# A first-weight split moved between x rows, a feed-forward block's weight sums moved into the projection before it, and a product split into the weights' old buffers

## The chip, the cores and the metric

The kernel runs on one core of a Trainium2 chip. The metric is the device time of one execution in microseconds (us); lower is better. The core has a matrix engine (TensorE, PE in the profile; its weight loads are PEld), three engines for elementwise work (VectorE = DVE, ScalarE = ACT, GpSimd = POOL) and a queue engine (SyncE = SP) that issues most DMAs. Each engine runs its own instructions in the order that the program gives it, and waits for the others through semaphores.

## The reference, cut to what matters

One encoder layer over 512 positions and 16 meta tokens, 1024 channels, all in float32:

```
h    = rmsnorm(x) ; proj = h @ w_in            # 40 column blocks of 128
a    = neighbourhood attention(proj) @ w_na_out
b    = differential attention(proj) @ w_diff_out
m    = sigmoid(g_na) * a + sigmoid(g_df) * b
x    = x + m @ w_o                             # "output projection"
h    = rmsnorm(x)
x    = x + (silu(h @ w_gate) * (h @ w_up)) @ w_down    # D_FF = 2816 = 22 * 128
out  = rmsnorm(x)[:, N_META:]
```

## The kernel before, in words

Activations lie transposed: channels on the 128 partitions, positions along the free dimension. Every float32 operand is split into a rounded high part and the remainder (`hi` by a cast on ACT, `lo` by a subtraction on DVE: `split`, lines 154 and 155; `wsplit`, lines 117 and 118, for weights), and `mm3` multiplies three times, high by high, high by low, low by high (lines 140, 142, 144).

**Order.** The kernel is written in Tile, which traces the Python program, then orders the instructions of each engine by a simulation of its own: the place in the program is a priority, and an engine takes the first instruction in that order whose inputs and whose buffers are there. So an instruction may run well ahead of its place in the code. Once ordered, an engine keeps its order on the chip. A tile of a pool shares `bufs` slots with the others of its tag; a new tile waits until a slot's last reader is done. `issue_after` pins a few instructions behind another one.

**Start** (`setup`). Column block 0 of `w_in` comes in two halves (`w0`) between the first rows of x (`xr`, eight rows of 128 channels). Each half is split (`wsplit(0, 2)`), and each x row is multiplied by the norm's gain into `xh` (ACT, line 244) and `xl` (DVE, line 245). The first dense block (tile `pk`) then runs over the rows k = 0 to 7: step k needs row k of `xh` and `xl`, and steps 4 to 7 need the second half of the weight. Two small loads (`lv` = the lambdas, broadcast to all partitions, and `mask`) are issued from POOL. `pq`, with the weight of block 1, follows `pk`.

**Weights of the dense part.** `wnext` hands out the splits of column blocks: loads three ahead into `wraw` (3 slots), splits one ahead into `whi`/`wlo` (2 slots each).

**Output projection** (`phase_b`, loop over m = 0 to 7, tile `po`). After each m: `x1[m]` gets the product added (line 854), `x_operands` makes the split operands of the feed-forward's left side (`xbh`, `xbl`, from `xg` and `xt`; line 998 and lines 1003 to 1015), `sum_sq` adds the square of `x1[m]` to `ssq` (squares on ACT, adds on POOL, the last on DVE).

**Feed-forward, gate and up** (22 blocks f). Each block forms two 512 x 128 by 128 products per half with seven multiplications of half size instead of eight (a Strassen-Winograd scheme; operands PB11, PB21, PB22, PT1 to PT4, tiles `pa`, `pb`, `pc`). `f_load(f)` loads gate weights into `fG` (a `wraw` slot) and up weights into `fV`, `fW`; `f_prep(f)` makes the sums of them and splits four operands: g = gate (`whi`/`wlo`), w (`fwh`/`fwl`, 2 slots), s (`fsh`/`fsl`, 1 slot), d (`fdh`/`fdl`, 1 slot). `f_products(f)` issues the seven products; in block 0 the mean of squares (`ms`, line 181) stands in product PT4. `glu` forms `g[f]` = silu(gate) * up. In the loop f, the preparation of block f + 1 is written ahead of the products of block f.

**Down projection** (tile `pdn`). `gh`, `gl` are the split of the 22 `g`; blocks (0, k) and (1, k) alternate over k, then m = 2 to 7. The pieces of `w_down` are split by `d_ahead`: the first two into `whi`/`wlo`, the others into a ring that takes the place of `xbh`/`xbl` (`wring`). Before, the 22 `gh` are a pool of their own (`GH`) opened when the pool of the feed-forward weights (`F`) is closed.

## Time and profile before

| | us |
|---|---|
| median of 3 runs (772.54 to 774.10) | 773.04 |
| the profiled execution, its own time | 773.11 |
| its span, first to last instruction | 771.3 |
| PE busy in the span | 748.6 |
| DVE / ACT / POOL busy | 575.6 / 379.7 / 55.3 |

The profile page lists busy time by engine, the span in slices, the chain of work that ended last, and groups of instructions. Beside it there is the timeline: start, duration, engine, line, operation, output tile <- input tiles, shape, count of merged instructions; in brackets, the idle time of the engine just before, and what ended it. The windows view gives busy time (and number of instructions) per engine in a stretch, and the granted TensorE clock as a share of full speed (PEclk).

### The profile page before, as it was taken

The page shows a single profiled execution, that of the slowest core. Times are in us where ns is not written, and L with a number is a line of the kernel's source. Part 1 is how long each engine was busy: PE and PEld are TensorE (multiplying, and loading weights), DVE is VectorE, ACT ScalarE, POOL GpSimd, SP SyncE. Part 2 cuts the span into 40 slices and gives each one's busy share as a digit, 9 for nine tenths or more (in the row PEclk, how much of TensorE's full clock was granted, in tenths as well). Part 3 has the DMA queues.
Part 4 walks back from the last instruction along what each step waited for, and adds up shares of the span by engine and source line. Part 5 has one row for each costly group of instructions (what it writes and reads, how often), then busy time and mean ns, then how long its engine had stood idle before and what let it go on. Part 6 is the DMA issues. An engine that isn't in the chain of part 4 may idle for free.

```text
span 771.3 us, 12598 instructions
## 1 busy us (share of the span) xinstructions
PE 748.6 (97%) x4794; PEld 674.1 (87%) x4794; DVE 575.6 (75%) x1053; ACT 379.7 (49%) x669; POOL 55.3 (7%) x141
## 2 busy tenths in 40 slices
PE   7999999999999999999998999999999989999995
PEld 5899889998889888878887999999999987888884
DVE  5777897788788867648889899999999959632214
ACT  6345545545554546514554655555555556422201
POOL 2030110110011000001121000000000000000100
PEclk8999999999999999999998999999999999999998
DMA  7474643453563412235541333333333232633003
GB/s 261 136 182 143 158 123 103 123 152 104 137 159 101 121 58 80 82 110 163 169 132 42 110 110 110 110 107 104 104 104 108 66 102 68 206 103 95 1 1 109
DMA packets 34715, 87.88 MB, mean 114 GB/s; under 512 B 4512, under 2 KB 6576, under 8 KB 34656
## 3 DMA queue, kind: packets, MB, share of 16 engines
q1 hardware_dynamic: 32688, 82.97, 35.6%
q0 software_dynamic: 1136, 3.34, 1.5%
q8 instruction: 37, 0.61, 0.3%
q10 hardware_dynamic: 832, 0.79, 0.3%
q14 instruction: 22, 0.18, 0.1%
HBM read 70.01 MB, written 2.10 MB: 93 GB/s over the span
## 4 chain that ended last, share of the span: by engine, by line
PE 85%; DVE 9%; DMA 2%; issue 1%; ACT 1%; SPq 0%; DVEq 0%; ACTq 0%
PE pdn L144 4%; PE pdn L140 4%; PE pdn L142 4%; PE pa L140 4%; PE pa L144 4%; PE pb L140 4%; PE pg L140 4%; PE pa L142 4%; PE pb L142 4%; PE pb L144 4%; PE pg L144 4%; PE pg L142 4%; PE s L513 2%; PE pv L140 2%; PE pv L142 2%; PE pv L144 2%
## 5 line engine op out<-in xcount | busy, mean ns | idle before, releaser
L117 ACT CAST whi<-wraw 128x1024 fp32r<-128x1024 f32 (+1 forms) x57 | 58.9, 1033 | 56.9 <-PE pd L142 13.1
L118 DVE TENSOR_TENSOR wlo<-wraw,whi 128x1024 fp32r<-128x1024 f32 (+1 forms) x57 | 68.5, 1201 | 17.2 <-ACT whi L117 16.9
L144 PE MATMUL pdn<-gh,wring 128*128 128x512 f32 x138 | 53.8, 390 | 1.3 <-DVE wring L155 1.3
L140 PE MATMUL pdn<-gh,wring 128*128 128x512 f32 x138 | 53.8, 390 | 0.0
L142 PE MATMUL pdn<-gl,wring 128*128 128x512 f32 x138 | 53.7, 389 | 0.0
L140 PE MATMUL pg<-xh,whi 128*128 128x512 f32 x128 | 52.6, 411 | 0.4 <-DVE vt L379 0.4
L142 PE MATMUL pg<-xl,whi 128*128 128x512 f32 x128 | 50.6, 395 | 0.0
L144 PE MATMUL pg<-xh,wlo 128*128 128x512 f32 x128 | 50.2, 393 | 0.0
L155 DVE TENSOR_TENSOR wring<-draw,wring 128x1024 fp32r<-128x1024 f32 (+1 forms) x22 | 24.7, 1126 | 28.8 <-ACT wring L154 28.8
L154 ACT CAST wring<-draw 128x1024 fp32r<-128x1024 f32 (+1 forms) x22 | 21.0, 974 | 45.9 <-PE pdn L142 34.5
L154 ACT CAST fdh<-fG 128x1024 fp32r<-128x1024 f32 x22 | 23.2, 1056 | 36.8 <-PE pa L142 34.7
L154 ACT CAST ath<-tp 128x256 fp32r<-128x256 f32 (+1 forms) x48 | 20.5, 443 | 42.2 <-PE tp L637 22.0
L1137 POOL TENSOR_TENSOR ssq<-ssq,sq 128x512 f32<-128x512 f32 x11 | 16.4, 1493 | 345.6 <-ACT sq L1136 335.2
L155 DVE TENSOR_TENSOR wlo<-fG,whi 128x1024 fp32r<-128x1024 f32 x22 | 26.9, 1224 | 14.4 <-ACT whi L154 14.4
L517 ACT ACTIVATE e<-s,m 128x528 f32<-128x528 f32 x32 | 22.5, 704 | 23.0 <-DVE m L515 22.7
L144 PEld LDWEIGHTS pdn<-gh,wring 128*128 128x128 f32 x138 | 25.9, 188 | 7.1 <-DVE wring L155 1.7
L140 PE MATMUL pk<-xh,whi 128*128 128x256 f32 (+1 forms) x128 | 28.9, 303 | 3.1 <-ACT xh L244 3.1
L140 PEld LDWEIGHTS pdn<-gh,wring 128*128 128x128 f32 x138 | 25.9, 188 | 5.6 <-ACT wring L154 0.2
L142 PEld LDWEIGHTS pdn<-gl,wring 128*128 128x128 f32 x138 | 25.9, 188 | 5.3
L155 DVE TENSOR_TENSOR fwl<-fW,fwh 128x1024 fp32r<-128x1024 f32 x22 | 26.9, 1225 | 3.1 <-ACT fwh L154 3.1
L144 PEld LDWEIGHTS pg<-xh,wlo 128*128 128x128 f32 x128 | 24.0, 188 | 5.2
L621 ACT ACTIVATE en<-en,m 128x272 f32<-128x272 f32 x32 | 16.7, 522 | 24.1 <-DVE m L619 23.8
(292 smaller groups left out, 2596.2 us busy)
## 6 DMA issues: line engine op xcount, KB each, us to landing
wraw<-in_w_in_dram SPq DMA_DIRECT2D x39, 512.0 KB, 3.8
fG<-in_w_gate_dram SPq DMA_DIRECT2D x22, 512.0 KB, 3.5
kd<-khl SPq DMA_DIRECT2D x32, 264.0 KB, 4.2
draw<-in_w_down_dram SPq DMA_DIRECT2D x16, 512.0 KB, 3.6
fW<-in_w_up_dram SPq DMA_DIRECT2D x22, 256.0 KB, 2.6
fV<-in_w_up_dram SPq DMA_DIRECT2D x22, 256.0 KB, 2.9
qs<-qhl SPq DMA_DIRECT2D x32, 128.0 KB, 2.8
wraw<-in_w_o_dram SPq DMA_DIRECT2D x8, 512.0 KB, 3.5
```

What stands on the lines that cost most here:

```text
L117: nc.scalar.copy(hi[:, k:k + h], raw[:, k:k + h])
L118: eng.tensor_tensor(out=lo[:, k:k + h], in0=raw[:, k:k + h], in1=hi[:, k:k + h].bitcast(F32), op=ALU.subtract)
L140: nc.tensor.matmul(outs[i], wh, rhs[i][0], start=start, stop=False, **kw)
L142: nc.tensor.matmul(outs[i], wh, rhs[i][1], start=False, stop=False, **kw)
L144: nc.tensor.matmul(outs[i], wl, rhs[i][0], start=False, stop=stop, **kw)
L154: self.nc.scalar.copy(hi, src)
L155: self.nc.vector.tensor_sub(lo, src, hi.bitcast(F32))
L513: nc.tensor.matmul(sc[:, r0:r1], qs[:, q], kd[:, p, r0:r1], start=p == 0, stop=p == 1)
L517: nc.scalar.activation(e, sc, AF.Exp, bias=m, accum_out=l[:, c:c + 1])
L621: x = nc.scalar.activation(e[:, :n], e[:, :n], AF.Exp, bias=m, scale=-1.0, accum_out=l[:, 0:1])
L1137: (nc.gpsimd if m < n - 1 else nc.vector).tensor_tensor(out=ssq, in0=ssq, in1=sq, op=ALU.add)
```

## The change

1. **Start.** `wsplit` with several parts becomes a generator; the first half of weight 0 is split ahead of row 0 as before, the second half behind rows 0 to 2 (`if k % 3 == 0: next(first)`). `lv` and `mask` are loaded from SP, in their old place in the program, behind the rope tables.
2. **Block 0 in the output projection.** `f_load(0)` stands ahead of the loop over m, `f_load(1)` at m = 5 (before: m = 3 and m = 6). `f_prep` becomes a generator in four parts, in the order w, s, d, g (before: g, w, s, d); block 0's four parts are issued at m = 0 to 3. The sum for d is written over `V`, not over `G`. The squares of `x1[4..7]` and their adds stand behind the loop over m, the adds on DVE. The mean of squares moves from PT4 to PT3, the last product.
3. **End of a block.** The two sums that read `pa` and `pb` are a function of their own (`sums`), issued right behind the products in every block; in the last block the order is PT4, PB21, PT2.
4. **Down projection.** The pool `F` stays open; the 22 `gh` are views of tiles with the tags of the feed-forward weights (`fV`, `fW`, `fwh`, `fwl`, `fsh`, `fsl`, `fdh`, `fdl`). The splits of `g` are issued in groups: 0 to 3, then the first two weight pieces, 4 to 7, then four at each fourth k.

```diff
 # wsplit
+        def part(k):
             nc.scalar.copy(hi[:, k:k + h], raw[:, k:k + h])
             eng.tensor_tensor(out=lo[:, k:k + h], in0=raw[:, k:k + h], in1=hi[:, k:k + h].bitcast(F32),
                               op=ALU.subtract)
-        self.wt[i] = (hi, lo)
+        if parts > 1:
+            return (part(k) for k in range(0, nk, h))
+        part(0)
 # setup
-        self.wsplit(0, 2)
...
+        first = self.wsplit(0, 2)
         for k in range(KT):
+            if k % 3 == 0:
+                next(first, None)
...
-        nc.gpsimd.dma_start(lv, a["lam"].partition_broadcast(P))
+        nc.sync.dma_start(lv, a["lam"].partition_broadcast(P))
...
-        nc.gpsimd.dma_start(self.mask, a["mask"])
+        nc.sync.dma_start(self.mask, a["mask"])
 # phase_b, output projection
+            self.f_load(0)
+            prep = self.f_prep(0)
             for m in range(KT):
...
-                self.sum_sq(bt, ssq, x1[:, m], m, KT)
-                if m == 3:
-                    self.f_load(0)
-                if m == 6:
-                    self.f_prep(0)
+                if m < 4:
+                    self.sum_sq(bt, ssq, x1[:, m], m)
+                    next(prep, None)
+                if m == 5:
                     self.f_load(1)
+            for _ in prep:
+                pass
+
+            for m in range(4, KT):
+                self.sum_sq(bt, ssq, x1[:, m], m, nc.vector)
 # phase_b, blocks f
-                held.append((f, self.f_products(G, xbh, xbl, f, ssq)))
+                parts = self.f_products(G, xbh, xbl, f, ssq)
+                held.append((f, *self.sums(bt, *parts)))
 # phase_b, down projection
-            GH = top.enter_context(tc.tile_pool(name="GH", bufs=1))
-            gh = [GH.tile([P, T], F32R, name=f"gh{k}") for k in range(NF)]
+            gh = []
+            for tag, n, bufs in (("fV", 2, 2), ("fW", 2, 2), ("fwh", 2, 2), ("fwl", 2, 2),
+                                 ("fsh", 1, 1), ("fsl", 1, 1), ("fdh", 2, 1), ("fdl", 2, 1)):
+                for _ in range(bufs):
+                    t = self.F.tile([P, n, T], F32R, name="gh", tag=tag, bufs=bufs)
+                    gh += [t[:, i] for i in range(n)]
+            def split_g(k0, k1):
+                for k in range(k0, k1):
+                    gl.append(G.tile([P, T], F32R, name="gl", tag="g", bufs=NF + 1))
+                    self.split(gh[k], gl[k], g[k])
...
+            split_g(0, 4)
             self.d_ahead(2)
+            split_g(4, 8)
...
                 if k % 8 == 0:
                     self.d_ahead(k // 4 + 4)
+                if k % 4 == 0:
+                    split_g(len(gl), min(NF, len(gl) + 4))
 # f_prep
-        g = hilo(G, [P, 2, 4, P], ("whi", "wlo"), 2, self.wp)
 
         nc.vector.tensor_tensor(out=W[:, 1], in0=V[:, 0], in1=W[:, 0], op=ALU.add)
         w = hilo(W, [P, 2, 4, P], ("fwh", "fwl"), 2, F)
+        yield
 
         nc.vector.tensor_tensor(out=V[:, 1], in0=W[:, 1], in1=G[:, 0], op=ALU.add)
         s = hilo(V[:, 1], [P, 4, P], ("fsh", "fsl"), 1, F)
-
-        nc.vector.tensor_tensor(out=G, in0=G, in1=V, op=ALU.add)
-        d = hilo(G, [P, 2, 4, P], ("fdh", "fdl"), 1, F)
+        yield
+
+        nc.vector.tensor_tensor(out=V, in0=G, in1=V, op=ALU.add)
+        d = hilo(V, [P, 2, 4, P], ("fdh", "fdl"), 1, F)
+        yield
+        g = hilo(G, [P, 2, 4, P], ("whi", "wlo"), 2, self.wp)
 # f_products
-                if f == 0 and i == PT4:
+                if f == 0 and i == PT3:
...
-        for part in (p2, p6, p4) if f == 0 else (p4, p6, p2):
+        for part in (p2, p6, p4) if f == 0 else (p4, p6, p2) if f < NF - 1 else (p4, p2, p6):
 # sum_sq: (nc.gpsimd if m < n - 1 else nc.vector) becomes (eng or nc.gpsimd)
```

## The prediction, made before the changed kernel was built or run

> **What bounds the kernel now.** I read the page first: the engines' busy time and the chain of work that ended last.

> ```profile
> span 771.3 us, 12598 instructions
> PE 748.6 (97%) x4794; PEld 674.1 (87%) x4794; DVE 575.6 (75%) x1053; ACT 379.7 (49%) x669; POOL 55.3 (7%) x141
> PE 85%; DVE 9%; DMA 2%; issue 1%; ACT 1%; SPq 0%; DVEq 0%; ACTq 0%
> ```

> PE bounds the kernel, and the change removes no product. All that can be won lies in the 771.3 - 748.6 = 22.7 us in which PE is idle, and in the time in which it runs below full clock. So the second view is the windows: in steps of 10 us to find PE's gaps (row 540 shows a stretch without), then cut at the gaps.

> ```profile
> 5.96:10.44 4.48, 1.41 (x8) 0.95 (x7) 1.11 (x3) 1.31 (x3) 0.25 (x5) 0.91 0.94 297
> 10.44:16.02 5.58, 5.58 (x23) 5.28 (x24) 5.35 (x9) 5.58 (x10) 0.00 (x0) 0.50 1.03 410
> 408.10:418.20 10.10, 6.32 (x42) 5.67 (x42) 10.07 (x14) 4.92 (x7) 2.30 (x1) 0.88 0.26 79
> 418.20:422.60 4.40, 4.40 (x21) 4.40 (x22) 4.13 (x16) 1.48 (x3) 0.00 (x0) 0.50 0.00 0
> 540.00:550.00 10.00, 10.00 (x88) 10.00 (x87) 9.09 (x12) 5.79 (x10) 0.00 (x0) 1.00 0.35 116
> 623.20:633.20 10.00, 9.99 (x86) 9.78 (x84) 5.05 (x7) 4.01 (x7) 0.00 (x0) 1.00 0.37 107
> 633.20:650.00 16.80, 13.16 (x55) 10.15 (x56) 14.90 (x23) 14.72 (x26) 0.00 (x0) 1.00 0.08 23
> ```

> The columns are the window, PE, PEld, DVE, ACT and POOL busy (with instructions), PE clock, DMA share and GB/s. Three gaps belong to the change: the start (4.48 - 1.41 = 3.07 us idle, then 5.58 us at clock 0.50), the way from the output projection into block 0 (10.10 - 6.32 = 3.78 us idle, then 4.40 us at clock 0.50), and the way into the down projection (16.80 - 13.16 = 3.64 us idle). Together 10.5 of the 22.7 us. In the blocks between (row 540) PE has no gap, and DVE is at 9.09 of 10; a product of 256 columns takes 10.00/88 = 0.114 us there, one of 512 columns twice that, 0.227.

> **Part 1, the start.** Which wait ends last there is read from the timeline.

> ```profile
> 1.20 0.89 SPq L230 DMA_DIRECT2D xr<-in_x_dram  x2
> 2.60 4.74 SPq L230 DMA_DIRECT2D xr<-in_x_dram  x6
> 4.88 0.73 ACT L244 ACTIVATE xh<-xr,vec 128x528 fp32r<-128x528 f32 x1 [0.88 <-DMA vec<-in_vec_dram]
> 9.13 0.62 ACT L117 CAST whi<-wraw 128x512 fp32r<-128x512 f32 x1 [3.52 <-DMA wraw<-in_w_in_dram]
> 10.44 0.81 PE L140 MATMUL pk<-xh,whi 128*128 128x256 f32 x2 [3.07 <-ACT xh L244]
> 12.29 0.64 PE L140 MATMUL pk<-xh,whi 128*128 128x256 f32 x2
> 13.61 0.64 PE L140 MATMUL pk<-xh,whi 128*128 128x256 f32 x2
> 17.06 0.41 PE L140 MATMUL pk<-xh,whi 128*128 128x256 f32 x2
> 17.80 0.41 PE L140 MATMUL pk<-xh,whi 128*128 128x256 f32 x2
> 16.94 1.22 DVE L118 TENSOR_TENSOR wlo<-wraw,whi 128x1024 fp32r<-128x1024 f32 x1
> xr<-in_x_dram SPq DMA_DIRECT2D x1, 264.0 KB, 4.0
> xr<-in_x_dram SPq DMA_DIRECT2D x1, 264.0 KB, 7.2
> GB/s 0 0 0 66 287 328 373 285 266 289 170 103 124 109 219 267 365 400 405 407 409 424 417 424 405 396 429 415 408 429 432 352 229 213 107 41 0 0 106 197
> ```

> ACT stands from 5.61 to 9.13 in front of the second half of weight 0, and rows 1 to 7 are queued behind it. Row 1 (the second of the two issues, begun at about 1.67, 4.0 to landing) was there at 5.7; row 2 (issued at 2.60, 7.2 to landing) at 9.8. With the second half behind row 2, row 1 is split by 7.2 and PE goes from step 0 (ends at 7.37) straight into step 1, instead of at 10.44. Step 2 wants row 2. A step costs 13.61 - 12.29 = 1.32 us at half clock and 17.80 - 17.06 = 0.74 at full clock; `pk` ends at 17.80 + 0.74 = 18.5.

> The poorest outcome: row 2 still lands at 9.8 and the clock still stays low until 16.02. Step 2 begins at 9.8 + 0.73 = 10.5 and not at 12.29, 4.2 steps instead of 2.8 are done at 16.02, and 1.4 steps of 0.74 are won: 1.0 us. The best: the DMA rate falls from 289 to 103 to 170 GB/s between 5.0 and 7.0 (the slices are 0.5 us). I put that down to the two small POOL loads, which go behind the rope tables. Lost there are 2 us x (289 - 126) = about 330 KB, or 1.1 us at 289 GB/s, so the second half and row 2 land about 1.1 to 2 us earlier; PE's gap shrinks to under 1 us, the clock is not lost, and ACT and DVE set the pace (about 0.75 a row): `pk` ends near 14.3, a win of 4.2 us. What comes next late is the weight of `pq`: its `wlo` begins at 16.94 and ends at 18.16, which today is in time by 0.3 us and now would be waited for, unless its own load, later in the same queue, gains as much. I take 2.5 us, the middle between 1.0 and 4.2, because of that next wait. `lv` and `mask` cost SP two issues ahead of the next weight loads and their 1.1 us of transfer comes later, where `pv`'s weight has slack (PE reaches `pv` only after the 24 products of `pq`, 24 x 0.227 = 5.4 us): nothing, and up to 1 us if that cover is gone.

> [...] Here 3.07 us of idling were enough for 0.50, and it lasted 5.58 us. [...]

> **Part 2, from the projection into block 0.** The timeline at the transition:

> ```profile
> 408.03 1.22 DVE L1044 TENSOR_TENSOR fG<-fG,fV 128x1024 f32<-128x1024 f32 x1
> 409.17 1.78 DVE L155 TENSOR_TENSOR xb<-xg,xb 128x512 fp32r<-128x512 f32 x1
> 411.66 1.22 DVE L155 TENSOR_TENSOR fdl<-fG,fdh 128x1024 fp32r<-128x1024 f32 x1
> 412.80 0.95 DVE L155 TENSOR_TENSOR xb<-xt,xb 128x768 fp32r<-128x768 f32 x1
> 412.66 0.38 PE L140 MATMUL pc<-xb,fwh 128*128 128x256 f32 x1 [0.86 <-ACT xb L154]
> 413.67 0.68 DVE L854 TENSOR_TENSOR m<-m,po 128x512 f32<-128x512 f32 x1
> 414.38 0.72 ACT L998 ACTIVATE xg<-m,ng 128x512 f32<-128x512 f32 x1 [0.82 <-DVE m L854]
> 415.73 0.69 DVE L1137 TENSOR_TENSOR ssq<-ssq,sq 128x512 f32<-128x512 f32 x1
> 416.94 0.42 DVE L1011 SCALAR_TENSOR_TENSOR xt<-xt,xg 128x256 f32<-128x256 f32 x1
> 418.86 0.83 ACT L154 CAST xb<-xt 128x768 fp32r<-128x768 f32 x1 [2.73 <-DVE xt L1013]
> 416.48 1.87 PE L181 MATMUL ms<-ones_d,ssq 128*128 128x1 f32 x8 [2.17 <-DVE ssq L1137]
> 745.63 1.05 PE L181 MATMUL msa<-ones_d,ssq 128*128 128x1 f32 x8
> 391.80 1.06 ACT L117 CAST whi<-wraw 128x1024 fp32r<-128x1024 f32 x1 [1.08 <-PE po L142]
> ```

> The projection's last product is out at 408.3, but DVE adds it to x only at 413.67: before it stand the sum and split for d of block 0 (1.22 + 1.22), and a split that a running POOL add has stretched to 1.78. DVE is the bound here (10.07 of 10.10). The price today: 3.78 us idle; 4.40 us at half clock, in which 21 products ran that take 21 x 0.114 = 2.4 us at full clock, so 2.0 lost; and the eight `ms` products, 1.87 instead of 1.05. Sum 6.6 us.

> After the change block 0's sums and splits (by the rows of the same sizes, 0.69 for 512 and 1.22 for 1024 columns: w 0.69 + 1.22, s 0.69 + 0.69, d 1.22 + 1.22, g 1.22: 6.9 us of DVE) belong to m = 0 to 3, and the late squares' adds come behind everything. The add of x1[7] can follow at 408.4 or so. From there its chain (add 0.68, gain 0.72, three sums of 0.42, cast 0.83, remainder 0.95) is about 5 us to the last operand, and ssq, four adds of 0.69 later, is ready after some 8 us. PE has for cover: PB11 and PT1 and three quarters of PB21, PT2 and PT4, each product 12 x 0.114 = 1.4 us, so 2 x 1.4 + 3 x 1.05 = 6.0 us before it needs x1[7], and 8.4 us before PT3 asks for ssq. Both covers exceed their chains: the loss of 6.6 falls to about 0.5. POOL loses three adds, DVE gains three of 0.69 under that cover.

> But g takes one of the two `whi`/`wlo` slots at m = 3 and keeps it until block 0's PB21, which needs x1[7]. From then on weights 5, 6 and 7 of the projection share one slot: the split of weight m + 1 can begin only when PE has finished m (today's row at 391.80 shows such a split beginning one whole block ahead). That is a cast of 1.06 and a remainder of 1.22, less the two products of 0.23 that need only the high part: about 1.9 us at each of three boundaries, 5.8 us. What hides it: PE's order is made by a simulation that fills holes with later work (`pc` above ran ahead of its place), and PB11 and PT1 of block 0 need only x1[0..3]: 2.8 us ready at the first boundary, and quarters of PB21, PT2, PT4, PB22 (0.35 each) as x1[4] and x1[5] come. That work is then missing as cover behind x1[7], where block 1's PT1 and PT4, whose w has two slots, must replace it. I price the held slot between 0 and 5.8, and take 1.5, nearer to the filled end since the trace shows such filling. Part 2: 6.6 - 0.5 - 1.5 = 4.6 us won.

> **Part 3, steady blocks.** No operation is added; in-place d and the order w, s, d, g are new. d's slot is free only when the block before ends, and d is used from 7.0 us into its block; 1.06 + 1.22 after the start it is there. DVE's 0.9 us of slack in 10 stay. Zero, with a bound in the rivals.

> **Part 4, into the down projection.**

> ```profile
> 633.89 0.73 PE L140 MATMUL pdn<-gh,dhi 128*128 128x512 f32 x2 [0.71 <-ACT gh L154]
> 636.28 0.50 PE L142 MATMUL pdn<-gl,dhi 128*128 128x512 f32 x1 [1.65 <-DVE gl L155]
> 635.53 12.56 DVE L155 TENSOR_TENSOR gl<-g,gh 128x512 fp32r<-128x512 f32 x16
> 649.28 0.50 PE L144 MATMUL pdn<-gh,wring 128*128 128x512 f32 x1 [1.29 <-DVE wring L155]
> ```

> `gh` waits for the pool of the weights to close, so nothing is split before 633.2; then DVE runs 16 `gl` in a row and the ring's remainder comes late. With `gh` in the weights' slots the first eight can be split in the last block, where DVE is busy 5.05 and ACT 4.01 of 10 us: 8 x 0.69 = 5.5 of DVE against 5 free, about seven in time. Behind 633.2 DVE then owes 2.7 (last block's sums) + 2 x 1.22 (ring) + one `gl` = 5.8 us up to k = 8, and PE takes 8 x 6 x 0.227 = 10.9 us to get there. All of 0.71 + 1.65 + 1.29 = 3.65 should go; I leave 0.35 for the first. Won: 3.3 (between 2 and 3.65).

> **Sum.** 2.5 + 4.6 + 3.3 = 10.4 us off the profiled execution's 773.11 (span 771.3 and 1.8 around it), which lies 0.07 above the median of 773.04: 762.6.

> **Rivals.**
> - *The clock is kept at the start* (above): 4.2 instead of 2.5: 760.9. For it: the gap gets short. Against: the first steps come spaced by data, and `pq`'s weight.
> - *The held slot is not filled*: PE stands 1.9 us at three boundaries: 4.3 more, 766.9. For it: the simulated order must place the filling to within some tenths. Against: `pc`'s running ahead.
> - *DVE takes the freed time back*: at 10.07 of 10.10 another split is late at x1[7], part 2 wins 1 instead of 4.6, and part 1 only 1.0: 767.7. Against: 6.9 us of work leave that stretch.
> - *Slower*: g is prepared last but used first (PB11). If an engine kept the written order, g's cast would stand behind d's, which waits for the end of the block before; PE would then wait at each of 21 block starts for two casts of 1.06 and a remainder of 1.22, some 2.3 to 3.3 us, 50 us in all: over 800. It decides from (10.4 + 1.5)/21 = 0.6 us a block. Against: g's input and slot are free half a block earlier, and an engine takes what is ready.
> - *Nothing happens*: the order was simulated, so instructions may already run where they are now written: 773. Against: the three gaps come from slots, a pool's closing and a queue's order, which the change does alter.

> **Chances.** Forecast (759.5 to 766) 0.50; clock kept 0.15; slot not filled 0.20; DVE takes it back 0.06; slower 0.05; nothing 0.04. Times within 0.2% (1.5 us), about what a measurement of this kernel can tell from no change, count as the same: faster 0.91, same 0.04, slower 0.05. The range reaches from the clock kept with part 2 and part 4 in full (773.0 - 4.2 - 6.6 - 3.65 = 758.6) to the poor ends (773.0 - 1.0 - 0.8 - 2.5 = 768.7): 758 to 769.

> **What would show it.** At the start: row 1's cast of line 244 right behind row 0's, the second half's behind row 2's, PE's gap under 3 us, less time at clock 0.50. In the projection: `whi` from `fG` near 386, `po` waiting for `wlo` at three boundaries, or `pa` and `pb` products between the `po`. Behind it: x1[7] added within 1 us of the last `po`, clock 1.00 throughout, `ms` at about 1.05. In the blocks: PE 10.00 of 10. Before 633: seven or eight `gh` casts, and no gap at the first `pdn`. The prediction is wrong if the blocks show PE gaps, if the three boundaries are bare, or if the wait only moves to `pq` and `pv`.

## The result, and the profile after

The change makes the kernel slower: 784.60 us in the median (783.16 to 785.01, 4 runs) against 773.27 (772.54 to 774.10, 4 runs) for the kernel before on the same chip; ratio 1.0144, 95% interval 1.0130 to 1.0159. The profiled execution grew from a span of 771.3 to 783.2 us, by 11.9.

The page of the changed kernel, then its windows (PE, PEld, DVE, ACT, POOL busy, clock, DMA share, GB/s):

```profile
span 783.2 us, 12535 instructions
PE 753.2 (96%) x4794; PEld 673.4 (86%) x4794; DVE 578.0 (74%) x1056; ACT 375.3 (48%) x669; POOL 50.8 (6%) x136
```

```profile
6.00:12.00 6.00, 5.65 (x37) 4.67 (x36) 4.96 (x8) 5.23 (x10) 0.00 (x0) 1.00 1.03 387
390.00:400.00 10.00, 7.54 (x24) 5.50 (x24) 6.96 (x12) 4.07 (x6) 0.15 (x1) 0.83 0.35 122
414.00:424.00 10.00, 9.92 (x85) 9.68 (x84) 7.57 (x21) 6.33 (x12) 0.00 (x0) 1.00 0.01 2
510.00:520.00 10.00, 8.18 (x64) 7.92 (x64) 8.01 (x10) 4.60 (x9) 0.00 (x0) 0.94 0.33 99
540.00:550.00 10.00, 10.00 (x89) 10.00 (x88) 7.89 (x11) 4.55 (x9) 0.00 (x0) 1.00 0.32 107
640.00:650.00 10.00, 8.01 (x55) 7.20 (x54) 6.70 (x9) 9.24 (x16) 0.00 (x0) 0.92 0.17 43
```

The start's gap and the gap into block 0 are nearly closed (5.65 of 6, 9.92 of 10, clock 1.00 in both). But PE now stands still in the middle of the projection (390 to 400) and in the steady blocks (510 to 520), where it had no gap before, and the way into the down projection (640 to 650) still has its gap. What PE waits for says the same; here are the largest of its waits outside the start and the end (engine, tile, line, what it waited for: us in total, times, the longest; one of 0.9 before `pn` is the same in both kernels and is left out):

```profile
PE pa L144 <- ACT c L1104: 7.7, 8, 1.8
PE po L144 <- ACT whi L119: 2.7, 3, 0.9
PE po L148 <- DVE wlo L120: 2.0, 3, 1.1
PE pdn L146 <- DVE gl L159: 2.0, 1, 2.0
PE pb L144 <- ACT c L1108: 1.1, 3, 0.5
```

For a balance by stage I take from the timelines when PE starts the first product of `po`, `pdn` and `pdh` (the last, halved blocks of the down projection). All kernels of the study stand in one table (us of the profiled execution):

| kernel | start to `po` | `po` to `pdn` | `pdn` to `pdh` | `pdh` to end | span |
|---|---|---|---|---|---|
| before | 364.62 | 269.27 | 108.48 | 28.93 | 771.3 |
| after | 361.75 | 283.52 | 108.63 | 29.30 | 783.2 |
| e1, blocks undone | 362.07 | 269.41 | 108.92 | 29.30 | 769.7 |
| e2, g late | 361.26 | 277.84 | 108.37 | 28.83 | 776.3 |
| e3, both | 361.75 | 262.06 | 108.33 | 28.76 | 760.9 |
| e4, before with d over V | 364.22 | 283.31 | 108.50 | 28.97 | 785.0 |
| e5, g elsewhere | 361.50 | 265.52 | 108.79 | 29.29 | 765.1 |
| e6, three V buffers | 361.68 | 271.89 | 107.42 | 29.31 | 770.3 |
| e7, e3 with gl early | 361.20 | 261.80 | 104.74 | 28.86 | 756.6 |
| e8, before, split order | 363.49 | 270.43 | 108.48 | 28.70 | 771.1 |
| e9, before, lv and mask | 361.34 | 269.37 | 108.51 | 29.18 | 768.4 |
| e10, before, whole start | 361.28 | 270.31 | 108.50 | 29.31 | 769.4 |

After against before: the start won 2.87, `po` to `pdn` lost 14.25, the down projection lost 0.15, the end 0.37; together 11.9.

**How a buffer makes the blocks wait.** One cycle of the timeline of the changed kernel, with the instructions that hang together:

```profile
489.27 1.22 DVE L159 TENSOR_TENSOR fdl<-fV,fdh 128x1024 fp32r<-128x1024 f32 x1
490.52 0.33 SPq L1046 DMA_DIRECT2D fV<-in_w_up_dram  x1
493.68 0.69 DVE L1058 TENSOR_TENSOR fW<-fV,fW 128x512 f32<-128x512 f32 x1 [0.84 <-DMA fV<-in_w_up_dram]
494.40 1.05 ACT L158 CAST fwh<-fW 128x1024 fp32r<-128x1024 f32 x1 [2.11 <-DVE fW L1058]
495.37 0.61 ACT L158 CAST fsh<-fV 128x512 fp32r<-128x512 f32 x1
495.88 0.36 ACT L1104 COPY c<-pa 128x256 f32<-128x256 f32 x1
496.29 0.38 PE L144 MATMUL pa<-xb,fdh 128*128 128x256 f32 x1 [1.12 <-ACT c L1104]
```

Read it downwards. `fdl` is the last reader of V now that d lies in V; it ends at 490.49, and 0.03 us later SP can issue the next load of V. That lands at 493.68, so DVE's first sum for a later block starts 0.84 late, ACT's cast `fwh` of that sum finds ACT idle for 2.11, and behind the two casts in ACT's queue stands the copy of `pa` for which PE waits. The same cycle before:

```profile
482.80 0.68 DVE L155 TENSOR_TENSOR fsl<-fV,fsh 128x512 fp32r<-128x512 f32 x1
483.51 0.33 SPq L1025 DMA_DIRECT2D fV<-in_w_up_dram  x1
487.27 1.22 DVE L155 TENSOR_TENSOR fdl<-fG,fdh 128x1024 fp32r<-128x1024 f32 x1
```

There the load follows `fsl`, and is issued 4.98 us ahead of the end of that cycle's `fdl` instead of 0.03 behind it.

### The profile page after: what moved, and what is told of

Read it like the earlier page. It is cut to its first block, busy times and chain, and to the rows that moved or that the text cites. A ratio compares the mean times of both kernels' runs of the same rounds, so it can differ in the third digit from the quotient of the medians.

```text
span 783.2 us, 12535 instructions
## 1 busy us (share of the span) xinstructions
PE 753.2 (96%) x4794; PEld 673.4 (86%) x4794; DVE 578.0 (74%) x1056; ACT 375.3 (48%) x669; POOL 50.8 (6%) x136
## 5 line engine op out<-in xcount | busy, mean ns | idle before, releaser
L120 DVE TENSOR_TENSOR wlo<-wraw,whi 128x1024 fp32r<-128x1024 f32 (+1 forms) x57 | 68.5, 1201 | 13.6 <-ACT whi L119 13.3
L144 PE MATMUL pdn<-gh,wring 128*128 128x512 f32 x138 | 53.7, 389 | 0.0
L144 PE MATMUL pg<-xh,whi 128*128 128x512 f32 x128 | 52.6, 411 | 0.4 <-DVE vt L385 0.4
L158 ACT CAST fdh<-fV 128x1024 fp32r<-128x1024 f32 x22 | 23.2, 1053 | 39.0 <-DVE fV L1066 25.7
L158 ACT CAST fwh<-fW 128x1024 fp32r<-128x1024 f32 x22 | 23.2, 1053 | 28.3 <-DVE fW L1058 28.3
L1164 POOL TENSOR_TENSOR ssq<-ssq,sq 128x512 f32<-128x512 f32 x8 | 12.7, 1584 | 363.7 <-ACT sq L1163 352.7
L144 PE MATMUL pa<-xb,fdh 128*128 128x256 f32 x88 | 25.7, 292 | 7.7 <-ACT c L1104 7.7
L144 PEld LDWEIGHTS pdn<-gh,wring 128*128 128x128 f32 x138 | 25.9, 188 | 5.3
L933 DVE TENSOR_TENSOR t<-pdn,nR 128x512 f32<-128x512 f32 x7 | 4.8, 691 | 34.0 <-PE pdn L148 34.0
## 6 DMA issues: line engine op xcount, KB each, us to landing
kd<-khl SPq DMA_DIRECT2D x32, 264.0 KB, 4.1
```

The source lines that it names most:

```text
L120: eng.tensor_tensor(out=lo[:, k:k + h], in0=raw[:, k:k + h], in1=hi[:, k:k + h].bitcast(F32), op=ALU.subtract)
L144: nc.tensor.matmul(outs[i], wh, rhs[i][0], start=start, stop=False, **kw)
L158: self.nc.scalar.copy(hi, src)
L933: nc.vector.tensor_tensor(out=t, in0=pd[m], in1=nR2, op=ALU.mult)
L1164: (eng or nc.gpsimd).tensor_tensor(out=ssq, in0=ssq, in1=sq, op=ALU.add)
```

## The experiments

Of the changed kernel, parts were undone one at a time (e1, e2) and together (e3, on which e7 builds; e5 builds on e1); on the kernel before, single parts of the change were done alone (e4, e8, e9) and both parts of the start together (e10).

**e1: blocks 1 to 21 as before.**

```diff
+        if f > 0:
+            g = hilo(G, [P, 2, 4, P], ("whi", "wlo"), 2, self.wp)
         nc.vector.tensor_tensor(out=W[:, 1], in0=V[:, 0], in1=W[:, 0], op=ALU.add)
...
-        nc.vector.tensor_tensor(out=V, in0=G, in1=V, op=ALU.add)
-        d = hilo(V, [P, 2, 4, P], ("fdh", "fdl"), 1, F)
+        D = V if f == 0 else G
+        nc.vector.tensor_tensor(out=D, in0=G, in1=V, op=ALU.add)
+        d = hilo(D, [P, 2, 4, P], ("fdh", "fdl"), 1, F)
         yield
-        g = hilo(G, [P, 2, 4, P], ("whi", "wlo"), 2, self.wp)
+        if f == 0:
+            g = hilo(G, [P, 2, 4, P], ("whi", "wlo"), 2, self.wp)
```

> The changed kernel, with the weight sums of blocks 1 to 20 made as before: the order g, w, s, d, and d written over G; block 0 keeps the new order and d over V. Theory A (d over V keeps the slot of V until the remainder of d is out, so the next load of V starts too late, and the blocks pay for it): the blocks lose their waits of PE for c1 and c2, PE is back at 10.00 of 10 us between 500 and 600, and the time falls by the 13 us that the steady blocks cost, from 784.6 to about 772. Rival B (the blocks lose their time to something else that came with the change, such as the sums taken right behind a block's products): the gaps stay, 782 or more.

Measured: 770.35 us (768.81 to 771.52, 6 runs); ratio to before 0.9970 [0.9957, 0.9982]. `po` to `pdn` falls by 14.1 us. The waits for `c` are gone; those of the projection stay:

```profile
PE po L144 <- ACT whi L119: 2.7, 3, 0.9
PE po L148 <- DVE wlo L120: 1.8, 3, 1.1
```

This shows that the blocks' loss lies in the order w, s, d, g or in d over V, not yet in which. (The edit holds for every block but the first, 21 of the 22.)

**e2: block 0's g split behind m = 6.** The edit replaces `next(prep, None)` under `if m < 4` by `if m in (0, 1, 2, 6): next(prep, None)`.

> The changed kernel, with the split of block 0's g moved from behind m = 3 to behind m = 6, where it was before; w, s and d of block 0 stay with m = 0 to 2. Theory A (g holds one of the two slots of whi and wlo, so the weights 5, 6 and 7 share the other): the waits of po for whi and wlo at three boundaries go and the clock stays at 1.00 there; the projection is 8 us shorter, of which some 1 us comes back as DVE work at its end: about 777. Rival B (block 0's sums on DVE in the projection make the weights' remainders late, whatever the slot): the boundaries keep their waits, 782 or more.

Measured: 778.34 us (777.78 to 778.74, 4 runs), 6.3 below the changed kernel. The projection runs without a gap (row 390 of its windows), and of its waits one of 0.2 us is left:

```profile
390.00:400.00 10.00, 10.00 (x46) 8.29 (x45) 9.06 (x16) 5.48 (x10) 0.00 (x0) 1.00 0.37 113
PE po L148 <- DVE wlo L120: 0.2, 1, 0.2
```

**e3: both edits.**

> The edits of the two runs above together. If each removes its own loss, they add: 784.6 - 12.5 - 7.5 = about 765. If the two losses are one (each only takes up slack that the other also needs), the sum is less, 770 or more.

Measured: 762.51 us (761.93 to 763.49, 4 runs); ratio to before 0.9868 [0.9853, 0.9882]. Each edit removes its own loss, and together they win a little more than the sum of the two: 22.1 instead of 14.2 + 6.3. PE is idle for 0.45 us from 361 to 425 and never from 425 to 623:

```profile
361.00:425.00 64.00, 63.55 (x357) 55.36 (x356) 57.46 (x92) 38.48 (x61) 7.34 (x6) 1.00 0.37 122
425.00:623.00 198.00, 198.00 (x1694) 197.52 (x1694) 176.89 (x219) 122.97 (x200) 0.00 (x0) 1.00 0.33 106
```

**e4: d over V alone, on the kernel before.**

```diff
-        nc.vector.tensor_tensor(out=G, in0=G, in1=V, op=ALU.add)
-        d = hilo(G, [P, 2, 4, P], ("fdh", "fdl"), 1, F)
+        nc.vector.tensor_tensor(out=V, in0=G, in1=V, op=ALU.add)
+        d = hilo(V, [P, 2, 4, P], ("fdh", "fdl"), 1, F)
```

> The kernel before with one thing changed: d is written over V and not over G, in all 21 blocks, in the order of before (g, w, s, d). Theory A (the slot of V): 773.3 + 13 = about 786, with the same waits of PE for c1 and c2 as in the changed kernel. Rival B (the place of d is harmless, the order w, s, d, g is not): 773.

Measured: 786.79 us (786.77 to 789.08, 4 runs); ratio 1.0190 [1.0171, 1.0209], 14.0 us more. `po` to `pdn` grows by 14.0, as much as e1 took back (14.1): these two lines alone make a loss of that size, in the old order. Its largest wait of PE is the one of the changed kernel, and in the chain that ended last DMA has 7% where it had 2%:

```profile
PE 69%; DVE 15%; DMA 7%; ACT 5%; issue 4%; SPq 0%; ACTq 0%; DVEq 0%
```

```profile
PE pa L140 <- ACT c L1080: 7.4, 8, 1.3
```

**e5: e1 with block 0's g, still behind m = 3, in other buffers.** In e1's edit, the last line takes `("fwh", "fwl"), 2, F` for block 0.

> The kernel of e1 (blocks 1 to 20 as before), with block 0's g still split behind m = 3, but into the second buffers of fwh and fwl instead of whi and wlo. Block 1's w then has to wait for block 0's. Theory A (it is the slot that g takes from the projection's weights): the waits of po for whi and wlo go although DVE and ACT do the same work at the same time; e1's 770.4 falls by about 7 to 763, or 765 if block 1's late w costs something behind x1[7]. Rival B (the cast and remainder of g in the middle of the projection make the weights' splits late): the waits stay, 770.

Measured: 767.04 us (766.91 to 767.39, 4 runs), 3.3 below e1. Between 361 and 425 PE no longer waits for `whi` or `wlo`; its one wait there is

```profile
PE ms L185 <- DVE ssq L1168: 2.2, 1, 2.2
```

The casts and remainders of g run at the same place in the program as in e1, so it is the slot and not the work that costs. The time lies between e3 and e1: `po` to `pdn` is 3.5 us longer than in e3, more than the 2 that I had allowed for block 1's late w (its cast comes at 415.89 instead of 375.05). The trace shows where they go: the wait of 2.2 and, right behind it, half clock from 412.52 to 415.93. But between the last `po` and `ms` PE does eleven quarters of products in both kernels. What is late is `ssq`: DVE adds the last `po` to x1[7] 3.55 us after PE has finished it (0.63 in e3), because block 1's sum for d and a split stand before it (the third row is this addition):

```profile
406.74 1.22 DVE L1069 TENSOR_TENSOR fG<-fG,fV 128x1024 f32<-128x1024 f32 x1
407.88 0.95 DVE L159 TENSOR_TENSOR xb<-xt,xb 128x768 fp32r<-128x768 f32 x1
408.74 0.68 DVE L861 TENSOR_TENSOR m<-m,po 128x512 f32<-128x512 f32 x1
```

Whether the missing w of block 1 plays a part beside that is not shown.

**e6: three buffers for V, order and place as changed.**

```diff
-        V = F.tile([P, 2, 4, P], F32, name="fV", tag="fV", bufs=2)
+        V = F.tile([P, 2, 4, P], F32, name="fV", tag="fV", bufs=3)
...
-        c2 = G.tile([P, 2, H], F32, name="c2", tag="c2", bufs=2)
+        c2 = G.tile([P, 2, H], F32, name="c2", tag="c2", bufs=1)
...
-                    gl.append(G.tile([P, T], F32R, name="gl", tag="g", bufs=NF + 1))
+                    gl.append(gh.pop(0) if k == 0 else G.tile([P, T], F32R, name="gl", tag="g", bufs=NF))
```

(The list of `gh`'s buffers gets the third one of `fV`, and the pool of `g` one buffer less.)

> The changed kernel, with d over V and the order w, s, d, g kept, but three buffers for V instead of two (paid for by one buffer of c2 and by the first remainder of the down projection taking a free buffer). Theory A (d over V hurts only because V's buffer comes free too late for the next load): with a third buffer the load starts a block earlier, PE's waits for c1 and c2 go, and the time is about that of e1, 771. Rival B (the order w, s, d, g hurts by itself): 784. Rival C (one buffer of c2 is too few): the waits of PE move to c2's copies, over 775.

Measured: 772.74 us (771.30 to 774.92, 10 runs). Of the 14.1 us, 11.6 are gone with the order and the place of d untouched, so the cause is the buffer of V. What is left of the waits for `c` (2.6 us) may be the single buffer of `c2` or the order; I did not separate these.

```profile
PE pb L144 <- ACT c L1108: 1.8, 3, 0.8
PE pa L144 <- ACT c L1104: 0.8, 2, 0.5
```

**e7: e3 with the first four gl ahead of the last block's sums.**

```diff
                 parts = self.f_products(G, xbh, xbl, f, ssq)
+                if f == NF - 1:
+                    split_g(0, 4)
                 held.append((f, *self.sums(bt, *parts)))
...
-            split_g(0, 4)
             self.d_ahead(2)
```

(`gh` and `split_g` are defined ahead of the loop for that, each tile made when it is first used.)

> The kernel of e3, with the first four remainders gl written ahead of the last block's sums instead of behind them. Theory A (gl waits only because DVE has it queued behind the last block's sums and behind a dlo that waits for its load, and not for its data): DVE does four gl in its idle time before that dlo, the wait of pdn for gl of 2.0 us goes, 762.5 - 2 = 760.5. Rival B (the next operand, dlo or the ring, is as late): the wait only changes its name, 762.5.

Measured: 758.90 us (758.31 to 759.50, 4 runs); ratio to before 0.9818 [0.9803, 0.9834]: faster than both kernels, by 14 and by 26 us. The timeline of e3, where DVE stands idle ahead of a `dlo` with `gl` behind it:

```profile
617.00 0.69 DVE L1135 TENSOR_TENSOR g<-s,u 128x512 f32<-128x512 f32 x1
621.21 1.23 DVE L159 TENSOR_TENSOR dlo<-draw,dhi 128x1024 fp32r<-128x1024 f32 x1 [3.52 <-ACT dhi L158]
625.69 0.68 DVE L159 TENSOR_TENSOR gl<-g,gh 128x512 fp32r<-128x512 f32 x1
626.43 0.50 PE L146 MATMUL pdn<-gl,dhi 128*128 128x512 f32 x1 [1.98 <-DVE gl L159]
```

and of e7, where that idle time is filled:

```profile
616.80 2.50 DVE L159 TENSOR_TENSOR gl<-g,gh 128x512 fp32r<-128x512 f32 x4
620.40 1.23 DVE L159 TENSOR_TENSOR dlo<-draw,dhi 128x1024 fp32r<-128x1024 f32 x1 [1.10 <-ACT dhi L158]
```

The down projection is 3.6 us shorter, not 2: with four `gl` ahead, the later ones, which in e3 came one by one just behind PE's need, are early too.

**e8, e9, e10: the start on the kernel before.** e8 has the order of the split alone, e9 the two loads on SP's queue alone, e10 both.

> The kernel before with one thing changed: the second half of weight 0 is split behind three x rows; lv and mask stay on POOL's queue. My first part priced this at 1.0 us at the least if row 2 still lands at 9.8. Theory A (both edits of the start are needed): pq begins 1.0 to 2 us earlier than 18.53, and the time falls by as much, 771 to 772. Rival B (the order of the split is the whole gain): pq begins at 14 to 15, pv 3 us earlier, 770. Rival C (it is nothing without the DMA part): 773.

> The kernel before with one thing changed: lv and mask are loaded from SP's queue behind the rope tables and not from POOL's. ACT still has the second half of weight 0 ahead of row 1. Theory A (the two POOL loads hold up the rows and the second half, as the split order alone showed: there the second half still came at 8.97): the cast of the second half begins at 6 to 7.3 instead of 9.13, row 1 follows at once, PE's gap falls from 3.07 to about 1 us, the clock stays at 1.00, and pq begins at 14 to 15 instead of 18.53: nearly the whole gain of the start comes from the queue. Rival B (without the order of the split the DMA part alone is worth little): pq at 17 or later.

> The kernel before with the whole of the change's start (split order, lv and mask on SP) and nothing else. By the changed kernel's trace pq begins at 14.0 to 14.8 and the projection 2.9 us earlier. Theory A (the start's gain is kept to the end): 773 - 2.9 = 770. Rival B (as with the split order alone, the way into block 0 gives part of it back by a longer stretch at half clock): 771 to 772.

Measured: e8 772.24 us, ratio 1.0000 [0.9986, 1.0013]; e9 770.57, 0.9980 [0.9970, 0.9991]; e10 771.26, 0.9980 [0.9964, 0.9995] (10 runs each). The cast of the second half of weight 0 in e8 and in e9:

```profile
8.97 0.62 ACT L119 CAST whi<-wraw 128x512 fp32r<-128x512 f32 x1 [2.98 <-DMA wraw<-in_w_in_dram]
6.51 0.62 ACT L117 CAST whi<-wraw 128x512 fp32r<-128x512 f32 x1 [0.83 <-DMA wraw<-in_w_in_dram]
```

So moving the two loads is the whole gain of the start: `po` begins 3.28 us earlier in e9 and 3.34 in e10, 1.13 in e8. The order of the split is worth nothing once the load is early. The move has two sides, another queue and a later time (`lv` is issued at 7.89 in e9, at 2.32 before), and no run separates them. These are single executions; in the medians less is left, 1.7 us in e9 (770.57 against 772.25), 1.0 in e10 and 0.3 in e8. e8 wins 1.1 at the start and gives 1.2 back before `pdn` (270.43 against 269.27): its way into block 0 has the same 3.8 us of idle time, but is at half clock from 413.06 to 423.30 instead of 415.80 to 422.62 (the last section has what went ahead of such stretches). e10 loses 1.0 there, by idle time (4.9 instead of 3.8), and e9 does not, though its start is nearly the same; why these two differ there stays open.

## Why the prediction was wrong

I forecast 762.6 and a range of 758 to 769. By its own steps:

- **Part 1, right in size, by the rival's way.** 2.5 forecast, 2.87 measured (profiled executions). The clock stayed at 1.00, as the rival had it, and `pq` began at 13.99 instead of 18.53, 4.5 earlier; the next wait took 1.1 of it back, where I had put it (`pq` waits 0.74 for its `wlo`, and `pv` begins 3.4 earlier). But the working gave the order of the split a floor of 1.0 and saw the loads on POOL as an addition of 1.1 to 2 us. The order does win 1.1 when it is alone (e8), but the loads are all of the gain: moving them brought the second half 2.6 us earlier (9.13 to 6.51), and the order adds 0.06 to that (e10 against e9). The stretch at half clock that the prediction read as 5.58 us is longer than the window that it cut: it lasts from 9.61 to 16.44, 6.83 us, and begins 2.2 us into the gap of 3.07.
- **Part 2, the loss that goes: right.** 6.6 less 0.5 forecast; e3 against before is 269.27 - 262.06 = 7.21, of which 0.86 is the gap at the first `pdn` (from the start of the product before it 0.98 in the kernel before, 0.12 after), so 6.35.
- **Part 2, the held slot: mis-sized.** I took 1.5 between 0 and 5.8. e1 differs from e3 only in where g is split: 269.41 - 262.06 = 7.35, above my upper bound. Nothing filled the boundaries but a part of PB11, and two gaps of 0.91 and 1.10 close together were followed by half clock (392.43 to 395.84; clock 0.83 in the row 390 to 400), which my bound left out. I leaned on `pc` running ahead in the old kernel, which showed that the order can do it and not that it would there.
- **Part 3, "Zero": the step that turned the sign.** 14.1 us (after against e1). I put the steady blocks at nothing after asking only when d's own slot comes free and whether DVE has slack. Those were not what stopped PE. I did not ask who waits for V, the tile that d was moved onto: its load. Writing over a tile prolongs its life to the new last reader, here from `fsl` to `fdl`. My rival "slower" put the threshold at 0.6 us a block (the blocks lost 14.1/21 = 0.67), but with another mechanism, g's cast behind d's; the chance of 0.05 rested on refuting that one.
- **Part 4: mis-sized.** 3.3 forecast; 0.86 at the first `pdn` came and 0.15 was lost behind it: there the two waits of before, 1.65 and 1.29, gave way to one of 1.99 (`gl`, at 647.88) and 3.41 us at half clock. The step that failed is "about seven in time": `gh` were cast early, but the share of free time on DVE (5 of 10) says nothing on what stands first in its queue: no `gl` was done before the first `pdn`. e7 shows that the room was there: 0.86 + 3.59 = 4.5.

The balance: -2.87 (start) - 6.35 (way into block 0) - 0.86 (first `pdn`) + 7.35 (held slot) + 14.11 (V) + 0.15 + 0.37 = 11.9. That e3 comes out at 762.5, my number, is chance: it has neither the held slot's 1.5 nor most of Part 4's 3.3.

At two places in the traces ready work stood behind a late instruction of its engine: on ACT a copy of `pa` behind late casts, for which PE stood 1.12 us (496.29), and on DVE in e3 a `gl` behind a `dlo` for which DVE stood 3.52 us.

## What to carry to other kernels

Before an operation is written over another tile, look up which load waits for that tile and where its new last reader runs: the price here was not the operation's but the late load's (14.1 us in the blocks, with no operation added), and it appeared on an engine that has nothing to do with either, at an instruction queued behind the late one (PE waited 7.7 us for `c`). DVE's free share (5 of 10 us) did not mean that it did early work early: no `gl` was done before the first `pdn`; look at what stands at the head of the queue. When a part takes a slot from a two-slot ring, price it by the bare ring and by the clock (here 7.35 us against my 1.5), and count on filling only where the new order shows it.

## What the runs showed of the hardware

**A stop cost more than its idle time.** The steady blocks start every 9.80 us in the kernel before; after, nearly every second one takes 10.6 to 13.6, in all 13.4 more. The idle rows give 7.7 + 1.1 = 8.8. Counted from start to start each of the twelve stops (eleven of them in the idle rows) takes about 0.27 longer than its idle time (at 518.11: 1.82 idle, but 2.10 from the start of the product before to this one, and 0.22 on to the next, where a stream of these products has 0.115 each), and the one stretch at half clock 1.6. Of the 0.27, 0.165 is overlap that is lost: a product's row lasts 0.28, but in a stream the next one starts after 0.115.

**Half clock after short gaps.** This stop of 1.82 us was followed by 3.41 us at half clock, and so was the wait of 1.99 for `gl` at 647.88. The same wait of 1.98 in e3 was not, nor was a stop of 1.99 at the start of e8:

```profile
518.11 0.39 PE L144 MATMUL pa<-xb,fdh 128*128 128x256 f32 x1 [1.82 <-ACT c L1104]
515.31:518.72 3.41, 1.59 (x14) 1.38 (x13) 2.81 (x4) 2.50 (x4) 0.00 (x0) 1.00 0.00 0
518.72:522.13 3.41, 3.41 (x19) 3.41 (x18) 3.41 (x5) 0.85 (x2) 0.00 (x0) 0.50 0.23 77
625.18:628.59 3.41, 2.09 (x8) 1.43 (x9) 3.41 (x5) 3.41 (x5) 0.00 (x0) 1.00 0.06 5
628.59:632.00 3.41, 3.31 (x15) 2.26 (x14) 3.25 (x5) 1.48 (x3) 0.00 (x0) 1.00 0.79 232
10.42 0.51 PE L144 MATMUL pk<-xh,whi 128*128 128x256 f32 x2 [1.99 <-ACT xh L250]
```

**Two small loads ahead of the x rows.** `lv` and `mask` are 176 KB. The DMA view of the first 12 us shows the software queue of POOL in the kernel before and in e9 (packets, MB, share of 16 engines):

```profile
q0 software_dynamic: 112, 0.19, 11.7%
q0 software_dynamic: 32, 0.01, 0.9%
```

`lv` is issued at 2.32 us, behind the half weight (2.13) and ahead of most x rows. With these 80 packets and 0.18 MB more at the start, the cast of that half weight began 2.6 us later (9.13, against 6.51 in e9, where the two loads stand behind the rest in SP's queue). How they held it up is not shown.
